# A guard at the end of a logsumexp kernel: range checks on the chip and a branch to a second path

## The chip, the cores and the metric

The kernel runs on one core of one Trainium2 chip. The metric is the device time of one execution in microseconds (us). The engines are TensorE (PE, with its weight loads PEld), VectorE (DVE), ScalarE (ACT), GpSimd (POOL) and SyncE (SP, which issues most DMAs).

## What is computed

```python
def reference(x, bias):          # x: (8, 2048, 2048) float32, bias: (8, 256) float32
    B, S, D = x.shape
    H = bias.shape[0]
    Dh = D // H
    x_heads = x.reshape(B, S, H, Dh).transpose(0, 2, 1, 3)
    x_heads = x_heads + bias[None, :, None, :]
    x_tiled = np.repeat(x_heads, 2, axis=2)
    mx = x_tiled.max(axis=-1, keepdims=True)
    lse = mx.squeeze(-1) + np.log(np.exp(x_tiled - mx).sum(axis=-1))
    return lse.astype(np.float32)          # (8, 8, 4096)
```

x and bias are drawn from a normal distribution. Each of the 16384 rows of x has 8 heads of 256 columns. For each head the kernel needs the log of the sum of exp(x + bias), and writes it twice. x is 134 MB, the result 1 MB.

## The kernel before

The kernel takes no maximum: it sums exp(x + bias) as it is and takes the log of the sum.

x comes in 64 tiles of 2 rows per partition (128 x 2 x 2048 numbers, 2 MB), 8 tiles to a batch. Four buffers (`xbs`) hold two tiles each. Tiles up to 41 are loaded in pairs (4 MB, L158), later ones alone, the last ones in pieces (L170). All loads are issued by SP, and the load of tile t + 8 waits until tile t's last users (`last_uses`, mostly DVE's reduce, L401) are done.

Every engine issues its instructions in the order in which the program writes them (`manual_schedule`). `STAGES` sets how a tile's heads are shared out.

- BULK (tiles 0 to 53). PE adds the bias to heads 0 to 2 in PSUM (L267 puts the bias there, L326 adds x through the identity). ACT takes exp of head 0 with its sum (L337) and of heads 1 and 2 (L344). POOL adds the bias to heads 4 to 7 in place (L376: 128x2048 numbers, x and `b_rep`, both in SBUF). ACT takes exp of heads 3 to 7 (L382). For heads whose exp was taken without the bias, DVE multiplies by exp(bias) (L394; the factors `w_ps` lie in PSUM). DVE then sums heads 1 to 7 (L401).
- MIXED (tiles 54 to 56) and the prompt stages (57 to 63). DVE multiplies by exp(bias) and sums one head at a time (L417, factors in `one_ps` and `w_ps` in PSUM, and once in `w_sb` in SBUF). POOL folds one or two heads (L433 multiplies by `w_sb`, L441 adds halves), and DVE sums what is left of them (L447).

The sums of batch b go to `R[b]`, 128 x 4 x 8 x 8 numbers of SBUF, 128x128 in all; those of the last batch to `R_last`. Two tiles after the last tile of a batch, `finish(b)` has PE transpose `R[b]` into the PSUM tile `tp` (L461) and ACT take the log into `res` (L471). After the seventh batch `store()` issues one store for seven batches (L475). At the end `finish_last()` transposes `R_last` (L482), takes the log (L488) and stores it (L489). Behind it, drains and semaphores close the program (L623).

The loop's end is where the change's calls hang:

```python
        fb, at = divmod(t - 2, NBLK)
        if fb >= 0 and at == NBLK - 1:
            finish(fb)
            if fb == B - 2:
                store()
    flush(for_pe)
    flush(for_pool)
    finish_last()
```

At loop step t DVE has been given the reduce of tile t - 1, so `finish(b)` comes on DVE behind the reduce of the tile that follows the batch.

The start: ACT loads the bias as one row (`brow`, L199), SP issues the first loads, POOL splits the bias into three bf16 parts (L208 to L212), ACT issues three small loads of them (L214), and DVE copies the spread bias to `b_rep` (L225).

Of the kernel before, what the change touches and what calls it, by code (L numbers as in the profile page):

```python
# [9 lines left out]
F32 = mybir.dt.float32  # L10
BF16 = mybir.dt.bfloat16
ACT = mybir.ActivationFunctionType
ALU = mybir.AluOpType
# [9 lines left out]
NEARLY = 5  # L23

NWARM = 3

# [27 lines left out]
def kernel(  # L56
# [6 lines left out]
    nc = tc.nc  # L63
    P = nc.NUM_PARTITIONS
    B, S, D = x.shape
    H, Dh = bias.shape
# [13 lines left out]
    sb = ctx.enter_context(tc.tile_pool(name="sb", bufs=1))  # L80
# [7 lines left out]
    ident = sb.tile([P, P], F32, name="ident")  # L88
# [2 lines left out]
    b3 = sb.tile([3, CPE], BF16, name="b3")  # L91
    bparts = sb.tile([1, 3, CPE], BF16, name="bparts")
    brest = sb.tile([1, 2, CPE], F32, name="brest")

    R = [sb.tile([P, KB, H, NB], F32, name=f"R{b}") for b in range(B - 1)]
    R_last = sb.tile([P, H, NBLK, K], F32, name="R_last")
    res = sb.tile([H * NB, B - 1, P, KB, 2], F32, name="res")
    res_last = sb.tile([P, P, 2], F32, name="res_last")
    xbs = [sb.tile([P, KB, D], F32, name=f"xb{i}") for i in range(NBUF // TB)]
# [6 lines left out]
    ps = [p[:, c : c + MM] for p in pairs for c in (0, MM)]  # L106
# [5 lines left out]
    def pieces(t):  # L112

        if len(modes_of(t)) == 1:
            return [(0, K, 0, D)]
        cols = [[(0, D)]] * K if t < T - 1 else LAST_COLS
        return [(k, k + 1, c0, c1) for k in range(K) for c0, c1 in cols[k]]
# [16 lines left out]
    def on_x(t, ins, after):  # L134
        buf = users[t // TB % len(xbs)]
        for t_u, u in buf:
            same = u.ins.engine == ins.ins.engine
            if u not in after and (not same or t_u % NBUF == t % NBUF and t_u < t):
                tc.declare_no_dep(
                    ins.ins,  # L140
                    u.ins,
                    reason="another tile, or waited for by those it waits for",
                )
        buf.append((t, ins))
        return ins
# [5 lines left out]
    def load(t):  # L151
        if TB <= t < BLOCKS:

            if t % TB == 0:
                after = [u for i in range(TB) if t >= NBUF for u in last_uses[t + i - NBUF]]
                ins = on_x(
                    t,
                    nc.sync.dma_start(  # L158
                        out=xbs[t // TB % len(xbs)], in_=rows_of(t, TB)
                    ),  # L160
                    after,
                )
                for i in range(TB):
                    loads[t + i, 0, 0] = ins
            return
        after = last_uses[t - NBUF] if t >= NBUF else []
        for k0, k1, c0, c1 in pieces(t):
            loads[t, k0, c0] = on_x(
                t,
                nc.sync.dma_start(  # L170
                    out=xts[t % NBUF][:, k0:k1, c0:c1],
                    in_=rows_of(t)[:, k0:k1, c0:c1],
                ),
                after,
            )
# [14 lines left out]
    for set_idx, (_name, funcs) in enumerate(get_activation_tables(nc.m.arch).items()):  # L190
        if ACT.Exp in funcs and ACT.Ln in funcs:
            nc.scalar.add_instruction(
                mybir.InstLoadActFuncSet(
                    name=nc.get_next_instruction_name(),
# [4 lines left out]
    nc.scalar.dma_start(out=brow, in_=bias.rearrange("h j -> (h j)").unsqueeze(0))  # L199
    for t in range(NBUF):  # L200
        load(t)
    nc.vector.memset(ones, 1.0)
    nc.vector.memset(ones3, 1.0)
    make_identity(nc, ident)

# [35 lines left out]
    n_ps = [0]  # L241
# [73 lines left out]
    def keep_warm():  # L315
        for _ in range(NWARM):
            nc.tensor.matmul(  # L317
                tp[:, 0], lhsT=ident, rhs=ident, start=True, stop=True
            )
# [45 lines left out]
    def each_row(src, c, n, k_rows):  # L365

        return bass.AP(
            tensor=src.tensor,
            offset=src.offset + c,
            ap=[src.ap[0], [0, k_rows], [1, n]],  # L370
        )
# [57 lines left out]
    def fold(t, k, h0, h1, sums, after):  # L429
# [24 lines left out]

        return add_up

    def finish(b):

        nr = H * NB
        for k in range(KB):  # L460
            nc.tensor.transpose(  # L461
                out=tp[0:nr, k],
                in_=R[b][:, k].rearrange("p h n -> p (h n)"),
                identity=ident,
            )
        tv = bass.AP(
            tensor=tp.tensor,
            offset=tp.offset,
            ap=[[tp.ap[0][0], nr], [1, P], [P, KB], [0, 2]],
        )  # L470
        nc.scalar.activation(out=res[:, b], in_=tv, func=ACT.Ln)  # L471
# [6 lines left out]
        )  # L478

    def finish_last():  # L480
        last = tp[:, KB - 1]
        nc.tensor.transpose(  # L482
            out=last, in_=R_last.rearrange("p h n k -> p (h n k)"), identity=ident
        )
        tv = bass.AP(
            tensor=last.tensor, offset=last.offset, ap=[last.ap[0], [1, P], [0, 2]]
        )
        nc.scalar.activation(out=res_last, in_=tv, func=ACT.Ln)  # L488
        nc.sync.dma_start(  # L489
            out=out[B - 1].rearrange("h (n r) -> (h n) r", r=2 * P),  # L490
            in_=res_last.rearrange("q p r -> q (p r)"),
        )


# [21 lines left out]
    def flush(later_work):  # L516
        for f in later_work:
            f()
        later_work.clear()

    for t in range(T):
        if t == T_FACTORS:
# [70 lines left out]
    flush(for_pe)  # L593
    flush(for_pool)
    finish_last()

    order.__exit__(None, None, None)

# [29 lines left out]
```

## Time and profile before

| what | value |
| --- | --- |
| time of three runs, us | 325.65, 325.32, 325.33 (median 325.33) |
| profiled execution: span from the first to the last instruction, us | 323.1 |
| median less that span, us (the page lists no other time of the profiled execution) | 2.2 |
| mean granted TensorE clock in it | 0.913 of full |
| read from and written to HBM, MB | 134.23, 1.05 |
| mean rate over the span, GB/s | 419 |
| POOL L376, 57 instructions, us busy | 257.6 |
| DVE L401, 56 instructions, us busy | 214.5 |
| ACT L382, 77 instructions, us busy | 157.1 |

How to read it: the page gives the busy time and the share of the span of each engine, then the span in 40 slices, where a digit is the busy share in tenths. Groups of instructions have a count, the busy time in us, the mean in ns of one, and the idle time of the engine before them with what ended it. In the chain of waits each line is a start in us, a length in us, and the engine, tile and line that the end of the program was waiting for at that time; "issue" is time in which the engine waited for nothing that the profile shows. In a timeline the first number is the start and the second the length.

### The profile page before, as it was taken

The numbers are of one execution on the slowest core, as the hardware profiler recorded it, in microseconds if no ns is written. First come the engines' busy times: TensorE is split into PE (matmuls) and PEld (weight loads), VectorE is DVE, ScalarE is ACT, GpSimd is POOL, SyncE is SP. The second block draws the span as 40 slices with busy tenths as digits, with TensorE's granted clock in tenths as the row PEclk, the third lists the DMA queues.
The fourth block names the chain that finished last, engine by engine and source line by source line (L and its number), as shares of the span: only waits on it lengthen the run. The fifth ranks groups of instructions, "written<-read, shape, count | busy, mean of one in ns | idle before, by whom it ended". The sixth has DMA issues, their size and how long they took to land.

```text
span 323.1 us, 2398 instructions
## 1 busy us (share of the span) xinstructions
PE 270.3 (84%) x691; PEld 102.9 (32%) x691; DVE 283.9 (88%) x306; ACT 265.8 (82%) x426; POOL 287.7 (89%) x120
## 2 busy tenths in 40 slices
PE   5999999889978769977869886888997786599984
PEld 2333333333323223322323322333333232035442
DVE  1037779999999998999899899898999999999995
ACT  1148679889869976988888978889998998899995
POOL 6939998999999999999999999999999999858874
PEclk9979799979979996998997997997999999559998
DMA  8999999999999999999999999999999999999995
GB/s 311 457 402 454 450 400 439 450 402 446 438 414 446 432 418 443 430 422 447 422 426 441 422 434 442 404 426 430 432 422 431 430 428 425 416 422 421 419 401 170
DMA packets 8830, 135.42 MB, mean 419 GB/s; under 512 B 1041, under 2 KB 1425, under 8 KB 2417
## 3 DMA queue, kind: packets, MB, share of 16 engines
q1 hardware_dynamic: 8720, 135.27, 98.6%
q8 instruction: 5, 0.08, 0.1%
q14 instruction: 7, 0.06, 0.0%
q10 hardware_dynamic: 98, 0.01, 0.0%
HBM read 134.23 MB, written 1.05 MB: 419 GB/s over the span
## 4 chain that ended last, share of the span: by engine, by line
DMA 40%; POOL 18%; ACT 17%; PE 14%; DVE 9%; issue 0%; SPq 0%; DVEq 0%
DMA xb<-in_x_dram 40%; POOL xb L376 18%; ACT xb L382 11%; DVE R L401 6%; PE pair L326 5%; PE one_ps L326 3%; PE pair L267 3%; ACT xb L357 2%; PE one_ps L267 2%; DVE xb L417 2%; PE pair L219 1%; ACT xb L337 1%; DVE xb L394 1%; ACT res L471 1%; ACT xb L344 1%; DMA brow<-in_bias_dram 1%
## 5 line engine op out<-in xcount | busy, mean ns | idle before, releaser
L376 POOL TENSOR_TENSOR xb<-xb,b_rep 128x2048 f32<-128x2048 f32 x57 | 257.6, 4539 | 20.7 <-DMA xb<-in_x_dram 20.6
L401 DVE TENSOR_REDUCE R<-xb 128x14 f32<-128x3584 f32 (+1 forms) x56 | 214.5, 3830 | 1.9
L382 ACT ACTIVATE xb<-xb 128x2560 f32<-128x2560 f32 (+5 forms) x77 | 157.1, 2050 | 10.3 <-POOL xb L376 10.1
L326 PE MATMUL pair<-xb,ident 128*128 128x512 f32 x216 | 114.3, 656 | 0.0
L326 PE MATMUL one_ps<-xb,ident 128*128 128x512 f32 x108 | 67.5, 710 | 11.5 <-DMA xb<-in_x_dram 11.5
L344 ACT ACTIVATE xb<-pair 128x1024 f32<-128x1024 f32 x54 | 55.5, 1027 | 23.2 <-PE pair L326 23.0
L326 PEld LDWEIGHTS pair<-xb,ident 128*128 128x128 f32 x216 | 46.2, 214 | 61.3 <-issue 61.3
L394 DVE TENSOR_TENSOR xb<-xb,w_ps 128x512 f32<-128x512 f32 x54 | 36.7, 681 | 26.2 <-ACT xb L382 26.2
L337 ACT ACTIVATE xb<-one_ps 128x256 f32<-128x256 f32 x108 | 40.0, 380 | 6.6 <-PE one_ps L326 6.6
L267 PEld LDWEIGHTS <-ones 3*128 3x128 bf16 (+1 forms) x192 | 16.9, 95 | 80.8 <-issue 71.4
L267 PE MATMUL one_ps<-b,ones 3*128 3x512 bf16 x49 | 18.6, 380 | 25.4 <-ACT xb L337 25.3
L267 PE MATMUL pair<-b,ones 3*128 3x512 bf16 x98 | 29.0, 375 | 0.0
L326 PEld LDWEIGHTS one_ps<-xb,ident 128*128 128x128 f32 x108 | 17.2, 200 | 33.9 <-DMA xb<-in_x_dram 18.0
L302 PE MATMUL pair<-xb,ident 128*128 128x512 f32 (+1 forms) x36 | 21.7, 689 | 5.7 <-DMA xb<-in_x_dram 5.7
L417 DVE CUSTOM_DVE_ANT_0 xb<-xb,w_ps 128x256 f32<-128x256 f32 x61 | 22.4, 418 | 0.0
L337 ACT ACTIVATION_READ_ACCUMULATOR xb<-one_ps 128x1 f32 x108 | 22.3, 207 | 0.0
L441 POOL TENSOR_TENSOR xb<-xb 128x128 f32<-128x128 f32 (+3 forms) x39 | 13.8, 355 | 3.1
L433 POOL TENSOR_TENSOR xb<-xb,w_sb 128x256 f32<-128x256 f32 (+1 forms) x13 | 10.0, 771 | 5.2 <-ACT xb L382 4.5
L317 PE MATMUL tp<-ident 128*128 128x128 f32 x84 | 13.7, 302 | 0.0
L317 PEld LDWEIGHTS tp<-ident 128*128 128x128 f32 x84 | 11.1, 200 | 3.5 <-issue 3.0
L357 ACT ACTIVATE xb<-pair 128x256 f32<-128x256 f32 x33 | 11.9, 364 | 0.0
L417 DVE CUSTOM_DVE_ANT_0 xb<-xb,one_ps 128x256 f32<-128x256 f32 x27 | 10.6, 415 | 0.1
(42 smaller groups left out, 83.4 us busy)
## 6 DMA issues: line engine op xcount, KB each, us to landing
xb<-in_x_dram SPq DMA_DIRECT2D x20, 4096.0 KB, 21.5
xb<-in_x_dram SPq DMA_DIRECT2D x17, 2048.0 KB, 22.7
xb<-in_x_dram SPq DMA_DIRECT2D x12, 1024.0 KB, 22.7
xb<-in_x_dram SPq DMA_DIRECT2D x4, 256.0 KB, 13.2
out_dram<-res SPq DMA_DIRECT2D x1, 896.0 KB, 6.7
xb<-in_x_dram SPq DMA_DIRECT2D x2, 384.0 KB, 15.8
xb<-in_x_dram SPq DMA_DIRECT2D x2, 128.0 KB, 6.3
out_dram<-res_last SPq DMA_DIRECT2D x1, 128.0 KB, 1.7
```

Of the source, the lines that this page charges most:

```text
L267: nc.tensor.matmul(p, lhsT=lhsT, rhs=each_row(b, h * Dh, Dh, K), start=i == 0, stop=False,)
L302: mm = nc.tensor.matmul(p, lhsT=ident, rhs=xts[t % NBUF][:, ka:kb, c : c + w], start=False, stop=True,)
L317: nc.tensor.matmul(tp[:, 0], lhsT=ident, rhs=ident, start=True, stop=True)
L326: mm = nc.tensor.matmul(p, lhsT=ident, rhs=xts[t % NBUF][:, :, h * Dh : (h + 1) * Dh], start=False, stop=True,)
L337: act = nc.scalar.activation(out=xts[t % NBUF][:, k, 0:Dh], in_=got[0][:, k * Dh : (k + 1) * Dh], func=ACT.Exp, accum_out=sums[:, k, 0:1],)
L344: act = nc.scalar.activation(out=xts[t % NBUF][:, :, Dh : m["pe"] * Dh].rearrange("p k (h j) -> p h k j", j=Dh), in_=got[-1].rearrange("p ...
L357: act = nc.scalar.activation(out=xts[t % NBUF][:, k, h * Dh : (h + 1) * Dh], in_=p, func=ACT.Exp, accum_out=sums[:, k, h : h + 1],)
L376: add = nc.gpsimd.tensor_tensor(out=v, in0=v, in1=each_row(b_rep, c - G0, D - c, k1 - k0), op=ALU.add)
L382: return on_x(t, nc.scalar.activation(out=v, in_=v, func=ACT.Exp), [after])
L394: mul = nc.vector.tensor_tensor(out=f, in0=f, in1=each_row(w_ps, m["pe"] * Dh - W0, n, k1 - k0), op=ALU.mult,)
L401: red = nc.vector.tensor_reduce(out=sums[:, k0:k1, h0:H], in_=v.rearrange("p k (h j) -> p k h j", j=Dh), op=ALU.add, axis=mybir.AxisListTy ...
L417: ttr = nc.vector.tensor_tensor_reduce(out=v, in0=v, in1=w, scale=1.0, scalar=0.0, op0=ALU.mult, op1=ALU.add, accum_out=dst,)
```

## The change

At the start the bias is loaded a second time, as 128 rows of 16 numbers, and DVE compares it with -32 and 32. In `finish(b)` DVE compares the 128x128 sums of the batch with 1e-12 and 1e18 and adds the outcome (1 where a value was changed by the clamp) to `bad`. In `finish_last()` it does the same for the last batch; PE counts `bad` and `out_of` over the partitions by two matmuls with a column of ones, and DVE sums the 128 counts to one number, `flag`. SP, ACT and DVE read `flag` into a register and branch. Where it isn't zero, `general()` computes all again with the maximum: 32 rounds, each loading 4 MB of x. With the inputs drawn here the sums and the bias lie inside the bounds.

```diff
+B_MAX = 32.0
+S_MIN, S_MAX = 1e-12, 1e18
+GB = 4
+GENERAL_B = 2
...
+    b_flat = sb.tile([P, D // P], F32, name="b_flat")
+    held = sb.tile([P, P], F32, name="held")
+    out_of = sb.tile([P, P], F32, name="out_of")
+    bad = sb.tile([P, P], F32, name="bad")
+    ones_k = sb.tile([P, 1], F32, name="ones_k")
+    flag = sb.tile([1, 1], F32, name="flag")
...
     nc.scalar.dma_start(out=brow, in_=bias.rearrange("h j -> (h j)").unsqueeze(0))
     for t in range(NBUF):
         load(t)
+    nc.scalar.dma_start(
+        out=b_flat, in_=bias.rearrange("h j -> (h j)").rearrange("(p c) -> p c", p=P)
+    )
     nc.vector.memset(ones, 1.0)
+    nc.vector.memset(ones_k, 1.0)
+    nc.vector.memset(bad, 0.0)
     nc.vector.memset(ones3, 1.0)
...
+    def outside(v, lo, hi, to):
+
+        c = held[:, 0 : v.shape[-1]]
+        nc.vector.tensor_scalar(
+            out=c, in0=v, scalar1=lo, scalar2=hi, op0=ALU.max, op1=ALU.min
+        )
+        nc.vector.tensor_tensor(out=to, in0=c, in1=v, op=ALU.not_equal)
+
+    def check_sums(r):
+        outside(r, S_MIN, S_MAX, out_of)
+        nc.vector.tensor_tensor(out=bad, in0=bad, in1=out_of, op=ALU.add)
+
     def finish(b):
 
+        check_sums(R[b].rearrange("p k h n -> p (k h n)"))
         nr = H * NB
...
     def finish_last():
+        r_last = R_last.rearrange("p h n k -> p (h n k)")
+        outside(r_last, S_MIN, S_MAX, out_of)
         last = tp[:, KB - 1]
         nc.tensor.transpose(
-            out=last, in_=R_last.rearrange("p h n k -> p (h n k)"), identity=ident
-        )
+            out=last, in_=r_last, identity=ident
+        )
+        count = ps[n_ps[0] % len(ps)][0:1, 0:P]
+        nc.tensor.matmul(count, lhsT=ones_k, rhs=bad, start=True, stop=False)
+        nc.tensor.matmul(count, lhsT=ones_k, rhs=out_of, start=False, stop=True)
...
         nc.sync.dma_start(
             out=out[B - 1].rearrange("h (n r) -> (h n) r", r=2 * P),
             in_=res_last.rearrange("q p r -> q (p r)"),
+        )
+        nc.vector.tensor_reduce(
+            out=flag, in_=count, op=ALU.add, axis=mybir.AxisListType.X
+        )
+
+    def general():
+
+        bias_all = xbs[GENERAL_B]
+        nc.sync.dma_start(
+            out=bias_all[:, 0],
+            in_=bass.AP(tensor=bias.tensor, offset=bias.offset, ap=[[0, P], [1, D]]),
+        )
...
+        for n, g in ((n, g) for n in range(S // P) for g in range(B // GB)):
...
+            nc.sync.dma_start(out=v, in_=xs[n, :, g * GB : (g + 1) * GB])
...
+    outside(b_flat, -B_MAX, B_MAX, bad[:, 0 : D // P])
 
     for t in range(T):
         if t == T_FACTORS:
...
     finish_last()
+    found = nc.values_load(
+        flag.bitcast(mybir.dt.int32),
+        engines=[mybir.EngineType.SP, mybir.EngineType.Activation, mybir.EngineType.DVE],
+        skip_runtime_bounds_check_because="only compared with zero",
+    )
+    with tc.If(found != 0, preferred_fallthrough_block=False):
+        general()
 
     order.__exit__(None, None, None)
```

In each round of `general()`, which is left out above, SP loads and stores, DVE adds the bias, takes the maximum, subtracts it and sums, and ACT takes exp and the log: on DVE five instructions a round, on ACT two, on SP two DMAs.

## What was predicted before the run

> **What bounds the kernel now.** I read the page first: busy shares and the slices.
>
> ```profile
> PE 270.3 (84%) x691; PEld 102.9 (32%) x691; DVE 283.9 (88%) x306; ACT 265.8 (82%) x426; POOL 287.7 (89%) x120
> ...
> DMA  8999999999999999999999999999999999999995
> ```
>
> The DMA engines are full from the second slice to the last but one, so the kernel is bound by reading x. Four compute engines are 82 to 89% busy under it: an instruction added to one of them is free only where that engine has a wait to give up. The change adds to VectorE (DVE) above all, so I went on to the waits, of the whole span, then of 230 to 304 us, then from 304 us.
>
> ```profile
> DVE xb L394 <- ACT xb L382: 26.2, 15, 12.6
> ```
> ```profile
> DVE xb L394 <- ACT xb L382: 0.2, 1, 0.2
> ```
> ```profile
> DVE R_last L447 <- POOL xb L441: 0.7, 4, 0.2
> ```
>
> Columns: waited in all, times, longest. DVE's 26.2 us are 12.6 before its first tile and 13.6 spread over the loop, yet in 230 to 304 us it waits once, 0.15 us at 230.25; after that it has its next work ready until 305 us. Then come four waits for POOL's folds (0.15, 0.20, 0.20, 0.19 us at 305.38, 307.46, 309.55, 311.63). So a delay of DVE before 230 us dies in a wait; one after 230 us is carried to 305 us, loses at most 0.74 us there, and goes on to the end. The chain of waits shows that DVE is the path from there:
>
> ```profile
> 312.54 1.60 ACT xb L382
> 314.14 0.02 issue
> 314.16 0.42 DVE xb L417
> ...
> 319.50 0.14 DVE R_last L447
> 319.64 0.14 issue
> 319.78 0.32 PE tp L482
> 320.09 0.02 issue
> 320.11 0.38 ACT res_last L488
> ```
>
> From 314.16 to 319.64 every link is DVE; then the transpose, Ln and the last store. At 314.16 DVE waits some 0.03 us for ACT's exp: 0.77 us of slack in all. Last, SP's own waits:
>
> ```profile
> SPq L489 <- ACT res_last L488: 6.5, 1, 6.5
> SPq L623 <- DMA out_dram<-res_last: 1.2, 1, 1.2
> ```
>
> The store is issued at 320.52, lands 1.7 us later (322.2), and the closing drains and semaphores end at 323.1, 0.9 us after the landing. While the store flies nothing else runs: cover of 1.7 us for anything that starts early enough.
>
> **The change part by part.** The sum is made against the profiled execution: span 323.1 us. The median of the three runs is 325.33, 2.2 us more, which I take as what lies around the span and leave alone.
>
> *The start.* Two memsets (0.165 us the like), a bias load of 128 rows of 64 bytes on ACT's queue and two compares on 128x16. DVE waits 12.57 us before its first tile at 21.15, and ACT until 9.45; both take this up. The three small loads behind it (L214) took 5.8 us to land and are first needed from the sixth tile on, after 38 us. Even if the bias needs as long, it is there by 8 us. Were the cover gone, it would cost about 1 us. The bytes: the like small queue (q10) shows 98 packets at 0.0%, so below 0.05% of 16 x 323 us, below 0.026 us each; 128 of them are below 0.2 us of DMA time. Taken as 0.
>
> *The checks.* Each of the seven finish() calls puts three 128x128 instructions on DVE: clamp, compare, add. The trace has none of that size, so by the neighbours:
>
> ```profile
> L394 DVE TENSOR_TENSOR xb<-xb,w_ps 128x512 f32<-128x512 f32 x54 | 36.7, 681 | 26.2 <-ACT xb L382 26.2
> L417 DVE CUSTOM_DVE_ANT_0 xb<-xb,w_ps 128x256 f32<-128x256 f32 x61 | 22.4, 418 | 0.0
> L447 DVE TENSOR_REDUCE R_last<-xb 128x1 f32<-128x32 f32 x12 | 2.2, 185 | 0.7 <-POOL xb L441 0.7
> ```
>
> From 681 ns for 512 columns and 418 for 256: 1.03 ns a column, so 418 - 132 = 286 ns for 128. The reduces agree: 185 ns for 32 columns plus 96 x 1.04 is 285. A dependent successor starts 0.03 us after the end (L394 to L401: 0.72 start to start for 0.69), an independent one 0.08 us before it (L417: 0.34 for 0.42). One check: 0.315 + 0.315 + 0.205 = 0.84 us. Bounds: 0.62 if all three overlap by 0.08; above, the port rival below.
>
> Where they fall: the check of a batch stands on DVE behind the reduce of the tile after it, so behind the L401 that end at 68.1, 104.5, 143.6, 181.8, 220.2 and 257.4 us; the seventh stands about 296.1 us among the L417. The first five meet waits of DVE (0.17 and 0.79 at 99.9 and 105.3, 2.01 at 130.0, 1.00 at 158.2, 0.31 to 0.79 at 172 to 183, 1.25 at 206.5, 0.79 at 221.0, 0.15 at 230.25) and die there. The loads wait for DVE's reduce, and one issued 0.84 us later lands no later: a 4 MB load lands 21.5 us after its issue (median), about 10 us of which are its own bytes at 419 GB/s, so about 11 us of older bytes stand before it. The sixth and the seventh have no wait behind them but the 0.77 us: 2 x 0.84 - 0.77 = **0.91 us** later on DVE at 314.16, hence at the store. Bounds: 0.47 (0.62 us a check) and 1.7 (slack gone).
>
> *The flag.* With the shift, the last L447 ends at 320.54. The transpose, Ln and store don't wait for what is new: issue 321.43, landing 323.1. Beside them: two more DVE instructions (0.03 + 0.286 + 0.03 + 0.286) to 321.17; the matmul that counts, priced as L482 (0.45 from DVE's end to PE's end) to 321.62; the reduce of 128 numbers, 0.03 + 0.285, to 321.94. Then SP, ACT and DVE each read the word into a register and branch. No row shows either. Below, a semaphore instruction of the closing block (0.02 us); above, the bias load at the start, 2.05 us from issue to landing (0.77 to 2.82). I take the middle, 1.0, as both are one round trip to a memory but the load also builds descriptors; for the branch 0.2, between 0.02 and 0.46 (the longest drain); and 0.2 for semaphores set right where the paths meet (some eight of 28 ns). That ends at 323.34, 0.24 later than the landing; bounds -1.1 (hidden: 0) and +1.4. Taken: **0.3 us**.
>
> Sum: 0.9 + 0.3 = +1.2 us, span 324.3, time **326.5 us**; with these bounds 325.8 to 328.4.
>
> On the flag the Trainium skill (Runtime: NRT & Kernel Launch, Instruction fetch mechanics) gives about 200 ns for a register loaded; as an estimate by that page the flag hides under the store and the time is 326.2. The same section warns that a taken branch to code outside the fetched window stalls; that is the second rival.
>
> **Rivals.**
> 1. *POOL stands in DVE's way.* Before the change, no DVE instruction of the main loop has both inputs in SBUF: L394 and L417 take weights from PSUM tiles (w_ps, one_ps). The sole exception:
>
> ```profile
> L417 DVE CUSTOM_DVE_ANT_0 xb<-xb,w_sb 128x256 f32<-128x256 f32 x1 | 0.4, 422 | 0.0
> ```
> ```profile
> 253.68 9.03 POOL L376 TENSOR_TENSOR xb<-xb,b_rep 128x2048 f32<-128x2048 f32 x2
> ```
>
> It starts at 319.07, POOL's last ends at 319.17, and it takes 422 ns as its kind does: 0.1 us of overlap, no sign of a wait, but little proof. The checks run wholly in SBUF while POOL is inside such 4.5 us instructions. Lighter form: each check waits once for the instruction that runs. At 257.4 that has 0.76 us left: 327.3 at least. With half an instruction (2.27) at each of six checks: 6 x 3.11 + 0.84 - 8.5 (DVE's waits from 99.9 on, 0.77 included) = 11.0, plus 0.3: 336.6. Heavy form: each of the three waits a whole POOL instruction: 0.76 + 2 x 4.54 + 0.84 = 10.7 a check; 6 x 10.7 + 0.84 - 8.5 = 56.5, DVE becomes the bound: 382. For: all three operands in SBUF, POOL 89% busy. Against: that one row.
> The Trainium skill (SBUF — State Buffer, Who interferes with whom) says DVE with two SBUF inputs, or in a mode using both ports, shares a port pair with GpSimd, and the later of the two is blocked fully until the other ends. By that page, as an estimate, the sum would be this rival's heavy form. The one overlapping row doesn't show it, and no other row here can.
> 2. *The branch waits for code.* The page's queues q8 and q14 bring instructions by DMA while the kernel runs. If the next code on SP, ACT or DVE isn't there, a small transfer's 2.05 us comes on top, once or twice: 328.6 to 330.6. For: 32 rounds of another path lie in the code. Against: the untaken path is asked to follow directly.
> 3. *Not slower.* The two late checks cost some 0.52 us each (0.206 for each that overlaps, the clamp half of that), and the flag hides under the store's 1.7 us. It decides if a check costs below 0.66 us and read and branch below 1.1 us: shift 0 to 0.55, 325.3 to 325.9.
> 4. *The other path runs after all.* Sums of 256 exponentials of normal numbers lie far inside 1e-12 to 1e18, a bias far below 32. It would read x again, 32 x 4 MB at 419 GB/s: over 320 us more.
>
> **How the numbers follow.** Forecast, 326.0 to 328.4: 0.42. Rival 2, to 330.6: 0.15. Rival 1 light, 327.3 to 336.6: 0.20; heavy, to 382: 0.13. Rival 3: 0.09; rival 4 or anything faster: 0.01. Leaving out the heavy form, rival 4 and the top of the lighter one, the range is 325.3 to 335. A measurement of this kernel can tell about 0.2% (0.65 us) from no change: slower 0.90, same 0.09, faster 0.01.
>
> **What would show it.** Right: clamp, compare and add rows of 0.2 to 0.3 us; no DVE wait from 257 to 305 us and fewer than four L447 waits after; the last L447 ends near 320.5; less than 0.5 us between the store's landing and SP going on. Wrong: rows of the checks lasting 1 to 5 us and ending with a POOL instruction (rival 1), POOL's L376 above 4.54; an empty stretch of 2 us or more behind the branch with an instruction packet in it (rival 2); a shorter SP wait for the store with the end unmoved (rival 3).

## The result and the profile after

The changed kernel takes 347.75 us (median of four runs, 346.52 to 348.04), the kernel before 325.32 us beside it. The ratio is 1.0675, with a 95% interval of 1.0655 to 1.0696: 22.4 us more, where 1.2 had been predicted, and above the predicted range (up to 335 us). The span is 345.8 us (323.1 before). So 22.7 us must be found in the trace. The lines of the loop have moved: L398 is POOL's addition of the bias (L376 before), L416 DVE's multiply (L394), L423 DVE's reduce (L401), L404 ACT's exp (L382), L469 DVE's small reduce of the tail (L447), L482 the clamp, L485 the compare, L489 the add.

The page after, its engines and the DMA slices:

```profile
PE 271.0 (78%) x695; PEld 103.0 (30%) x695; DVE 317.2 (92%) x334; ACT 263.5 (76%) x426; POOL 287.7 (83%) x120
...
DMA  8999999999999999999999999999999979999500
```

The other engines are as busy as before to within 2.3 us; DVE has 33.3 us more. The DMA slices are no longer all full: in the last quarter reading x waits for something. The chain of waits by engine says for what; the kernel before comes first, then the changed one:

```profile
DMA 40%; POOL 18%; ACT 17%; PE 14%; DVE 9%; issue 0%; SPq 0%; DVEq 0%
```
```profile
DVE 78%; PE 15%; ACT 4%; issue 1%; DMA 1%
```

The mean granted TensorE clock is lower too, 0.879 for 0.913, but PE is busy only 0.7 us longer and has 15% of the chain for 14%.

The groups of DVE by form show what the 33.3 us are (count, busy us, mean ns, idle time before them):

```profile
L482 DVE TENSOR_SCALAR held<-R 128x128 f32<-128x128 f32 x7 | 14.8, 2117 | 0.0
L489 DVE TENSOR_TENSOR bad<-bad,out_of 128x128 f32<-128x128 f32 x7 | 10.6, 1521 | 0.2
L485 DVE TENSOR_TENSOR out_of<-held,R 128x128 f32<-128x128 f32 x7 | 6.5, 935 | 0.2
...
L485 DVE TENSOR_TENSOR out_of<-held,R_last 128x128 f32<-128x128 f32 x1 | 0.3, 293 | 0.0
...
L482 DVE TENSOR_SCALAR held<-R_last 128x128 f32<-128x128 f32 x1 | 0.2, 227 | 0.1
```

The same clamp and compare, on the same size, take 227 and 293 ns on the sums of the last batch, when POOL has finished, and 2117 and 935 ns on average inside the loop. The seven checks take 14.8 + 10.6 + 6.5 = 31.9 us, 4.56 us each. That the profile counts it as busy time doesn't mean that DVE computes for so long: the 2 us are a stand inside an instruction that has started. To see what ends it, two checks on DVE's timeline and POOL's line beside them (start, length):

```profile
67.34 4.52 DVE L482 TENSOR_SCALAR held<-R 128x128 f32<-128x128 f32 x1
71.90 0.29 DVE L485 TENSOR_TENSOR out_of<-held,R 128x128 f32<-128x128 f32 x1
72.22 0.29 DVE L489 TENSOR_TENSOR bad<-bad,out_of 128x128 f32<-128x128 f32 x1
```
```profile
62.74 9.03 POOL L398 TENSOR_TENSOR xb<-xb,b_rep 128x2048 f32<-128x2048 f32 x2 [0.61 <-DMA xb<-in_x_dram]
72.40 4.55 POOL L398 TENSOR_TENSOR xb<-xb,b_rep 128x2048 f32<-128x2048 f32 x1 [0.63 <-DMA xb<-in_x_dram]
```

POOL's second instruction ends at 62.74 + 9.03 = 71.77 us, DVE's clamp at 71.86. POOL then waits 0.63 us for its next tile, and in that pause compare and add run at their own lengths. The fifth check meets a POOL that doesn't pause:

```profile
225.24 1.13 DVE L482 TENSOR_SCALAR held<-R 128x128 f32<-128x128 f32 x1
226.40 4.53 DVE L485 TENSOR_TENSOR out_of<-held,R 128x128 f32<-128x128 f32 x1
230.97 4.52 DVE L489 TENSOR_TENSOR bad<-bad,out_of 128x128 f32<-128x128 f32 x1
```
```profile
212.74 40.68 POOL L398 TENSOR_TENSOR xb<-xb,b_rep 128x2048 f32<-128x2048 f32 x9
```

Nine POOL instructions follow each other without a pause (4.52 us each), and now compare and add each last one of them. This check costs 10.2 us, from 225.24 to the start of the next multiply at 235.41.

The same holds in all the kernels below that have such instructions in the loop. Over seven profiles 62 of them last longer than 0.6 us, and each of the 62 ends 0.08 to 0.16 us behind the end of one of POOL's additions of the bias. DVE's own waits show what became of the cover that the prediction counted on:

```profile
DVE xb L416 <- ACT xb L404: 13.0, 5, 7.1
```

Before it was 26.2 us. 7.1 us of the 13.0 are before the first tile and the rest ends at 44.8 us; behind that DVE never waits in the loop, so all later delay is carried on. The last reduce of tile 55 ends at 309.8 us, 21.3 after that of the kernel before (288.5). The remaining 1.4 us arise behind it, nearly all behind the last store: from its issue to the end it is 3.77 us (2.62 before).

### The profile page after: what moved, and what is told of

It reads as the page before. It is cut to its first block, busy times and chain, and to the rows that moved or that the text cites. A ratio compares the mean times of both kernels' runs of the same rounds, so it can differ in the third digit from the quotient of the medians.

```text
span 345.8 us, 2458 instructions
## 1 busy us (share of the span) xinstructions
PE 271.0 (78%) x695; PEld 103.0 (30%) x695; DVE 317.2 (92%) x334; ACT 263.5 (76%) x426; POOL 287.7 (83%) x120
## 4 chain that ended last, share of the span: by engine, by line
DVE 78%; PE 15%; ACT 4%; issue 1%; DMA 1%
DVE R L423 52%; DVE xb L439 9%; DVE xb L416 8%; PE pair L348 6%; DVE held L482 4%; DVE bad L489 3%; PE one_ps L348 3%; PE pair L289 3%; ACT xb L404 3%; DVE out_of L485 2%; PE one_ps L289 2%; PE pair L241 1%; DVE R_last L423 1%; ACT xb L366 1%; DMA brow<-in_bias_dram 1%
## 5 line engine op out<-in xcount | busy, mean ns | idle before, releaser
L398 POOL TENSOR_TENSOR xb<-xb,b_rep 128x2048 f32<-128x2048 f32 x57 | 257.6, 4539 | 22.2 <-DMA xb<-in_x_dram 22.2
L423 DVE TENSOR_REDUCE R<-xb 128x14 f32<-128x3584 f32 (+1 forms) x56 | 214.5, 3830 | 1.9
L404 ACT ACTIVATE xb<-xb 128x2560 f32<-128x2560 f32 (+5 forms) x77 | 158.2, 2066 | 2.6 <-POOL xb L398 2.6
L348 PE MATMUL pair<-xb,ident 128*128 128x512 f32 x216 | 117.2, 671 | 0.0
L366 ACT ACTIVATE xb<-pair 128x1024 f32<-128x1024 f32 x54 | 56.9, 1054 | 18.8 <-PE pair L348 18.7
L416 DVE TENSOR_TENSOR xb<-xb,w_ps 128x512 f32<-128x512 f32 x54 | 36.7, 679 | 13.0 <-ACT xb L404 13.0
L359 ACT ACTIVATE xb<-one_ps 128x256 f32<-128x256 f32 x108 | 41.2, 402 | 5.8 <-PE one_ps L348 5.7
L289 PE MATMUL one_ps<-b,ones 3*128 3x512 bf16 x49 | 18.7, 382 | 21.3 <-ACT xb L359 21.3
L496 PE MATMUL tp<-ident,R 128*32 128x128 f32 x28 | 6.7, 335 | 35.4 <-DVE R L423 35.4
L506 ACT ACTIVATE res<-tp 32x1024 f32<-32x1024 f32 x7 | 7.1, 1012 | 33.5 <-PE tp L496 33.5
L455 POOL TENSOR_TENSOR xb<-xb,w_sb 128x256 f32<-128x256 f32 (+1 forms) x13 | 10.0, 772 | 21.9 <-ACT xb L404 21.3
L348 PEld LDWEIGHTS one_ps<-xb,ident 128*128 128x128 f32 x108 | 17.4, 203 | 25.4 <-issue 19.1
L359 ACT ACTIVATION_READ_ACCUMULATOR xb<-one_ps 128x1 f32 x108 | 24.8, 230 | 0.0
L324 PE MATMUL pair<-xb,ident 128*128 128x512 f32 (+1 forms) x36 | 18.4, 595 | 0.0
L463 POOL TENSOR_TENSOR xb<-xb 128x128 f32<-128x128 f32 (+3 forms) x39 | 13.8, 355 | 3.1
L482 DVE TENSOR_SCALAR held<-R 128x128 f32<-128x128 f32 x7 | 14.8, 2117 | 0.0
L496 PEld LDWEIGHTS tp<-ident,R 128*32 128x32 f32 x28 | 1.8, 101 | 40.3 <-DVE R L423 38.2
## 6 DMA issues: line engine op xcount, KB each, us to landing
xb<-in_x_dram SPq DMA_DIRECT2D x4, 256.0 KB, 10.7
```

The source lines that it names most:

```text
L289: nc.tensor.matmul(p, lhsT=lhsT, rhs=each_row(b, h * Dh, Dh, K), start=i == 0, stop=False,)
L324: mm = nc.tensor.matmul(p, lhsT=ident, rhs=xts[t % NBUF][:, ka:kb, c : c + w], start=False, stop=True,)
L348: mm = nc.tensor.matmul(p, lhsT=ident, rhs=xts[t % NBUF][:, :, h * Dh : (h + 1) * Dh], start=False, stop=True,)
L359: act = nc.scalar.activation(out=xts[t % NBUF][:, k, 0:Dh], in_=got[0][:, k * Dh : (k + 1) * Dh], func=ACT.Exp, accum_out=sums[:, k, 0:1],)
L366: act = nc.scalar.activation(out=xts[t % NBUF][:, :, Dh : m["pe"] * Dh].rearrange("p k (h j) -> p h k j", j=Dh), in_=got[-1].rearrange("p ...
L398: add = nc.gpsimd.tensor_tensor(out=v, in0=v, in1=each_row(b_rep, c - G0, D - c, k1 - k0), op=ALU.add)
```

## The theories and the experiments

The letters in the expectations: **P** is the first rival of the prediction, POOL stands in the way of the checks on DVE, which then is the bound. **B** says that the time comes with the branch and the second path's code. **C** says that PE and ACT, which keep the order in which the program is written, stand behind a late finish(), and that this multiplies the delay. Of P there are forms: that only instructions with two inputs in SBUF stand; or (P2, in the last kernels) that every DVE instruction wholly in SBUF but the reduces does, and that the clamp alone can stand over several POOL instructions. The kernel before was run beside each group of kernels: 325.43, 325.21 and 325.40 us.

### Without the seven checks

```diff
     def finish(b):
-        check_sums(R[b].rearrange("p k h n -> p (k h n)"))
```

The sums of the first seven batches are not compared with the bounds; the flag, the branch and the second path stay.

> The seven checks in the loop are left out (the sums of the first seven batches aren't compared); the bias check, the check of the last batch, the count, the flag and the branch stay. Theory P (a check's DVE instruction, with all operands in SBUF, stands until POOL's running instruction ends; DVE has no waits left after about 45 us, so 31.9 us of checks less some 8.5 us of waits reach the end): the checks were nearly all of it, what stays is the end: store to end 3.8 us in place of 2.6 us, so 326.5 to 327.2 us. Rival B (the branch, its second path's code and the flag cost it): 340 us or more.

Measured: 326.44 us (326.0 to 327.84), ratio 1.0032 (1.0019 to 1.0046), just below what P expected. Of 22.4 us some 21 go with 21 small DVE instructions. B falls as the main cause; what is left over the kernel before is about 1 us.

### Without the branch

```diff
-    found = nc.values_load(
...
-    with tc.If(found != 0, preferred_fallthrough_block=False):
-        general()
```

The checks and the flag are computed and nobody reads the flag; the second path isn't there.

> The checks stay, the flag is computed, but nobody reads it: register loads, branch and second path are left out. Theory P: only the end gets shorter, by the 1.2 us that it took over the store's landing: 346 to 346.8 us, with the same long check instructions. Rival B: back to within 5 us of the kernel before.

Measured: 345.55 us (345.18 to 345.92), ratio 1.0617 (1.0592 to 1.0642), 2.2 below the changed kernel. That is a little below the expected 346 to 346.8. The three groups of the checks take 31.0 us (13.8, 10.6 and 6.6) for 31.9; if that is 0.9 of the difference, the rest, 1.3 us, goes with the branch. B falls a second time, from the other side.

### The same checks when POOL is done

```diff
     def finish_last():
+        for r in R:
+            check_sums(r.rearrange("p k h n -> p (k h n)"))
...
```

(and no call in finish()).

> The same seven checks, instruction for instruction, all moved behind the last sum of the last batch, when POOL has nothing left to do. Theory P: each takes its own length, 0.23 + 0.29 + 0.29 us and gaps, so 21 instructions take about 6 us; they stand before the last batch's check but not before its store; with the end of 1.2 us, of which the store now hides more, 330 to 333 us. Rival C or a theory by which the instructions are slow by themselves (2.1 us the clamp, 1.5 us the add): 21 instructions of 32 us, 355 us or more.

Measured: 329.85 us (329.65 to 330.76), ratio 1.014 (1.0114 to 1.0167), just below what P expected. DVE's groups by form:

```profile
L485 DVE TENSOR_TENSOR out_of<-held,R 128x128 f32<-128x128 f32 x7 | 2.0, 292 | 0.2
L489 DVE TENSOR_TENSOR bad<-bad,out_of 128x128 f32<-128x128 f32 x7 | 2.0, 292 | 0.2
L482 DVE TENSOR_SCALAR held<-R 128x128 f32<-128x128 f32 x7 | 1.5, 219 | 0.0
```

The same 21 instructions on the same data take 5.5 us in place of 31.9, so neither their work nor the addresses make them long. They cost 3.4 us more than no checks at all (326.44), as the last store, issued at 319.04 us, flies beside part of the 5.5. PE, ACT and the loads are done there too, so this run alone doesn't name POOL; the ends of the 62 instructions do, and the next experiment keeps the place. The 3.4 us are the price of a place without POOL and without cover, a sixth of the loss.

### A reduce in place of clamp, compare and add

```diff
-        check_sums(R[b].rearrange("p k h n -> p (k h n)"))
+        r = R[b].rearrange("p k h n -> p (k h n)")
+        for i, op in enumerate((ALU.max, ALU.min)):
+            nc.vector.tensor_reduce(
+                out=ends[:, i, b : b + 1], in_=r, op=op, axis=mybir.AxisListType.X
+            )
+        if b == B - 2:
+            outside(
+                ends.rearrange("p i b -> p (i b)"),
+                S_MIN,
+                S_MAX,
+                bad[:, D // P : D // P + 2 * (B - 1)],
+            )
...
```

Per batch DVE takes the largest and the smallest sum of each partition, and compares these 14 columns once.

> Each check becomes two reduces on DVE, maximum and minimum of the same 128x128 sums into one column each, and the columns are compared once after the seventh batch. The reduces read one operand in SBUF. Theory P: they don't wait for POOL, 0.29 us each whatever POOL does; two late checks of 0.5 us less 0.77 us of slack reach the end, and the 1.2 us of the end: 326.5 to 327.5 us. Rival C (any DVE instruction put in at this place costs as much, since PE and ACT stand behind it with the transposes and the log): still 340 us or more, with PE waiting tens of us for the reduces as it does now (38 us at the transposes).

Measured: 326.69 us (326.27 to 328.62), ratio 1.0042 (1.0026 to 1.0058). The reduces read the same `R[b]` in the same places of the loop:

```profile
L496 DVE TENSOR_REDUCE ends<-R 128x1 f32<-128x128 f32 x14 | 3.3, 276 | 0.0
```

Fourteen of them, none longer than 279 ns, by the side of 2117 for the clamp; eleven run wholly inside one of POOL's additions. DVE's multiply, which writes 128x512 numbers to SBUF and has one operand in PSUM, is as unharmed: none of the 54 in the changed kernel lasts longer than 690 ns, and 34 lie wholly inside an addition of POOL. So it isn't SBUF, the place or `R` that stands in the way, but the kind of the instruction. This is the best version with the guard that was run.

### The reduces without the branch

The kernel above without the register reads, the branch and the second path.

> Maximum and minimum as before, but nobody reads the flag: register loads, branch and second path are left out. What is left is the reduces: 2 late checks of 0.5 us less 0.77 us of slack, so 0.2 to 0.4 us over the kernel before, 325.4 to 325.9 us; the branch itself is then worth 0.9 to 1.3 us of the 326.7 us. If the time stays at 326.5 us or more, the reduces or the start cost it and not the branch.

Measured: 325.74 us (325.27 to 327.59), ratio 1.0016 (1.0001 to 1.0031). Against their own runs of the kernel before, the reduces cost 0.3 us and the guard as a whole 1.3; so branch and flag are about 0.9 us of it.

### Marks in bf16 and an earlier count

```diff
-    out_of = sb.tile([P, P], F32, name="out_of")
-    bad = sb.tile([P, P], F32, name="bad")
+    out_of = sb.tile([P, P], BF16, name="out_of")
+    bad = sb.tile([P, P], BF16, name="bad")
...
-    ones_k = sb.tile([P, 1], F32, name="ones_k")
+    ones_k = sb.tile([P, 1], BF16, name="ones_k")
...
+        nc.tensor.matmul(count, lhsT=ones_k, rhs=bad, start=True, stop=False)
         last = tp[:, KB - 1]
...
```

This is meant to bring the flag of the kernel with the reduces forward.

> As the kernel with maximum and minimum, and with a shorter way to the flag: the marks and the column of ones are bf16, and the matmul that counts the earlier marks stands before the last transpose. Theory: the two counting matmuls took 1.2 us on PE with the last one ending 0.9 us after the last mark; with one pass each and only one of them late, the flag comes 0.5 to 0.8 us earlier and the end with it: 326 to 326.8 us. If the end doesn't move, something other than the flag sets it (the semaphores where the paths meet, or the store).

Measured: 326.76 us (326.19 to 328.2), ratio 1.0041 (1.0026 to 1.0055): no gain. In the profiles the time from the last store's issue to the end is 3.53 us for 3.72, so the flag came some 0.2 us earlier where 0.5 to 0.8 was expected; a difference of that size doesn't show in the times.

### finish() two tiles later

```diff
-        fb, at = divmod(t - 2, NBLK)
+        fb, at = divmod(t - 4, NBLK)
```

PE's transposes wait 35.4 us for DVE in the changed kernel and ACT's logs 33.5 us for PE; before, the logs waited 4.1. C makes these waits a cause; here they have two tiles of time.

> The checks as changed, but each finish (check, transposes, log) two tiles later. Rival C (the loss comes from PE and ACT standing in order behind transposes that wait for DVE's late sums, 38 us on PE): two tiles more give DVE 9 us to get there, most PE and ACT waits go, and the time falls by 8 us or more. Theory P: DVE is the bound from 45 us on without waits, so what PE and ACT wait for costs nothing: 345 to 350 us, PE's wait for the sums much smaller, the check instructions as long as before on average (they meet other POOL instructions, so a few us either way).

Measured: 347.47 us (346.91 to 348.79), ratio 1.0695 (1.0669 to 1.072). The checks take 31.3 us. PE's transposes now wait 11.6 us and ACT's logs 14.7, and the time stays: these waits come from DVE's stand and cost nothing of their own, and C falls.

### The checks on POOL

```diff
...
-        outside(r, S_MIN, S_MAX, out_of)
-        nc.vector.tensor_tensor(out=bad, in0=bad, in1=out_of, op=ALU.add)
+        c = held_g[:, 0 : r.shape[-1]]
+        nc.gpsimd.tensor_scalar(
+            out=c, in0=r, scalar1=S_MIN, scalar2=S_MAX, op0=ALU.max, op1=ALU.min
+        )
+        nc.gpsimd.tensor_tensor(out=out_g, in0=c, in1=r, op=ALU.subtract)
+        nc.gpsimd.tensor_tensor(out=out_g, in0=out_g, in1=out_g, op=ALU.mult)
+        nc.gpsimd.tensor_tensor(out=bad_g, in0=bad_g, in1=out_g, op=ALU.add)
...
+        nc.tensor.matmul(count, lhsT=ones_k, rhs=bad_g, start=False, stop=False)
```

Four instructions on POOL (clamp, subtract, square, add) take the place of the three on DVE; a difference that isn't zero counts as outside. In the loop DVE then has no instruction of the kind that stands.

> [...] POOL takes about 0.46 us for a 128x128 two-operand instruction in the trace, so 1.9 us a check, and waits 22 us in all for x. Theory P: DVE has no instruction that POOL can hold up; POOL's waits take the checks up: 326.5 to 328.5 us. Rival C: POOL is 83 to 89% busy too and stands before ACT, so most of 7 x 1.9 us comes through: 335 us or more.

Measured: 330.2 us (329.79 to 332.22), ratio 1.0171 (1.0136 to 1.0206), above what was expected. POOL's waits of the loop in this kernel:

```profile
POOL xb L402 <- DMA xb<-in_x_dram: 8.0, 4, 4.9
...
POOL held_g L493 <- DVE R L427: 1.9, 1, 1.9
```

POOL had 20.6 us of waits for loads before and gives up only 12.6 of them, for 13.6 us of instructions, their gaps and a wait for DVE's reduce: the waits of an engine are not all to be had. In this execution the last store is issued 2.4 us later than before (322.94 for 320.52). The other half of the loss lies behind the store: 5.06 us to the end where the changed kernel has 3.77 and the kernel before 2.62 (see the second rival below). The loss is 5 us instead of 22, as P has it.

### POOL's addition in halves

```diff
...
-        v = xts[t % NBUF][:, k0:k1, c:D]
-        add = nc.gpsimd.tensor_tensor(
-            out=v, in0=v, in1=each_row(b_rep, c - G0, D - c, k1 - k0), op=ALU.add
-        )
+        for k in range(k0, k1):
+            v = xts[t % NBUF][:, k : k + 1, c:D]
+            add = nc.gpsimd.tensor_tensor(
+                out=v, in0=v, in1=each_row(b_rep, c - G0, D - c, 1), op=ALU.add
+            )
...
```

If a check waits for the POOL instruction that runs, half as long an instruction should halve the wait.

> The checks as changed, but POOL's bias add of 128x2048 is split into two instructions of 128x1024 (2.3 us each). Theory P, that the wait is for the whole POOL instruction that runs: no check instruction lasts over 2.6 us (now up to 4.6 us), the checks' sum falls from 31.9 to between 14 and 22 us, the time to 330 to 340 us, if POOL's own total doesn't grow by more than 5 us. Rival D (the two engines share a port word by word, or DVE is slow at such operands by itself): check instructions keep their lengths, 345 us or more.

Measured: 359.21 us (357.09 to 360.56), ratio 1.1056 (1.103 to 1.1082): the opposite of what was expected. At 225 us it goes as P has it, with 2.36 and 2.33 us for compare and add where one POOL instruction takes 2.36. But the sixth check:

```profile
267.79 19.59 DVE L484 TENSOR_SCALAR held<-R 128x128 f32<-128x128 f32 x1
287.41 0.29 DVE L487 TENSOR_TENSOR out_of<-held,R 128x128 f32<-128x128 f32 x1
```
```profile
219.92 67.37 POOL L399 TENSOR_TENSOR xb<-xb,b_rep 128x1024 f32<-128x1024 f32 x29
```
```profile
L399 POOL TENSOR_TENSOR xb<-xb,b_rep 128x1024 f32<-128x1024 f32 x114 | 265.7, 2363 | 12.9 <-DMA xb<-in_x_dram 12.9
```

One clamp stands for 19.59 us, more than eight POOL instructions of 2.36 us, and is let go at 287.4 us. POOL's last instruction of an unbroken row of 29, from 219.92 us on, ends at 287.29; the check at 225 us, which was let in at each end, lies in the same row. So an end of a POOL instruction isn't always a door for DVE. The time alone would suit rival D of the expectation, but the lengths don't: the other eight long instructions of the loop last 1.8 to 2.4 us and each ends with one of POOL's. The checks take 41.5 us in all, 9.6 more than in the changed kernel, and the profiled execution is 9.6 us longer (357.09 for 347.54; the medians differ by 11.5). POOL itself does 8.1 us more work (265.7 for 257.6), as two halves take 2 x 2.363 = 4.73 us for 4.54.

### Three compares, or three clamps

```diff
-        outside(r, S_MIN, S_MAX, out_of)
-        nc.vector.tensor_tensor(out=bad, in0=bad, in1=out_of, op=ALU.add)
+        for c in (held, out_of, held):
+            nc.vector.tensor_tensor(out=c, in0=ident, in1=r, op=ALU.not_equal)
```
```diff
+        for c in (held, out_of, held):
+            nc.vector.tensor_scalar(
+                out=c, in0=r, scalar1=S_MIN, scalar2=S_MAX, op0=ALU.max, op1=ALU.min
+            )
```

The seven checks are replaced by instructions of one kind whose outcome nobody uses: three with two inputs in SBUF, or three with one.

> A check is three compares of the sums with the identity, two operands in SBUF each; clamp and add are left out, and nothing of the first seven batches is marked. Theory P2 (an instruction of this kind waits for the end of the POOL instruction that runs, never for a second one): no compare over 4.6 us; the first of a check waits for a rest, the others 0.29 us where POOL pauses or a whole instruction where it has work ready; sum 20 to 45 us, time 336 to 360 us. If only the clamp did harm: below 330 us.

> A check is three clamps, one operand in SBUF each and two constants; compare and add are left out, and nothing of the first seven batches is marked. Theory P2: the clamp waits for POOL as well, though it reads one operand, and it is the one that can miss the gap between two POOL instructions (19.6 us once where POOL's adds were halved): at least one clamp over 4.6 us, 340 us or more. If what counts is two operands in SBUF alone: 0.22 us each, below 328 us.

Measured: 342.01 us (341.78 to 342.66), ratio 1.0519 (1.0502 to 1.0537), with compares; 341.87 us (341.46 to 342.81), ratio 1.0506 (1.0488 to 1.0523), with clamps. The groups of the kernel with three compares come first, then those of the kernel with three clamps:

```profile
L489 DVE TENSOR_TENSOR held<-ident,R 128x128 f32<-128x128 f32 x14 | 21.0, 1503 | 0.0
...
L489 DVE TENSOR_TENSOR out_of<-ident,R 128x128 f32<-128x128 f32 x7 | 6.3, 898 | 0.0
```
```profile
L489 DVE TENSOR_SCALAR held<-R 128x128 f32<-128x128 f32 x14 | 22.8, 1628 | 0.0
L482 DVE TENSOR_SCALAR held<-b_flat 128x16 f32<-128x16 f32 x1 | 7.5, 7487 | 1.8 <-DMA b_flat<-in_bias_dram 1.8
...
L489 DVE TENSOR_SCALAR out_of<-R 128x128 f32<-128x128 f32 x7 | 5.9, 838 | 0.0
```

Both kinds stand alike, 27.3 and 28.7 us in all. That only two inputs in SBUF make an instruction stand falls: the clamp has one. None of the clamps of the checks lasts longer than 4.6 us, though P2 had expected one that does; only the clamp of the bias at the start does, on 16 columns, and there the cover of DVE's first wait hides it. Its row with POOL's above it, in the kernel with three clamps:

```profile
9.03 8.96 POOL L398 TENSOR_TENSOR xb<-xb,b_rep 128x2048 f32<-128x2048 f32 x2
10.54 7.49 DVE L482 TENSOR_SCALAR held<-b_flat 128x16 f32<-128x16 f32 x1 [1.76 <-DMA b_flat<-in_bias_dram]
```

It passes the end of POOL's first addition (13.52 us) and is let go at that of the second. So with whole additions too an instruction can stand over more than the one that runs. The same clamp lies in all thirteen changed kernels: in the five where POOL goes on without a pause it takes 7.4 to 7.6 us, in the eight where POOL pauses between its first two tiles, by 0.09 us or more, 2.2 to 2.8 us.

### Three compares beside the halves

Both edits together.

> The three compares, and POOL's bias add in two instructions of 128x1024 (2.36 us). Theory P2: no compare over 2.5 us, so the sum is at most 6 x 3 x 2.4 and likely 20 to 30 us, and the time lies below that of the three compares with whole adds by 3 us or more, without the 19.6 us that the clamp stood. If the wait isn't for one POOL instruction: some compares over 2.5 us, or no less time.

Measured: 356.28 us (356.08 to 359.48), ratio 1.0986 (1.0934 to 1.1038). The sixth check again:

```profile
267.43 19.62 DVE L491 TENSOR_TENSOR held<-ident,R 128x128 f32<-128x128 f32 x1
286.97 0.28 DVE L491 TENSOR_TENSOR out_of<-ident,R 128x128 f32<-128x128 f32 x1
```

A compare stands 19.62 us in the place where the clamp did, where 2.5 us at most had been expected, and the time is 14 us above that of the three compares with whole additions, not 3 below. P2 falls in this point: the clamp isn't special, and a second POOL instruction can be waited for. In both kernels with halves it is the first instruction of the sixth check that stands so long; what decides is open (see below).

## Why the prediction was wrong, step by step

**The step that failed is the price of one check**, "0.315 + 0.315 + 0.205 = 0.84 us", and with it the chances: the forecast got 0.42 and the rival that came about 0.33 in two forms. As a price of the instructions alone it was right: 219 + 292 + 292 = 803 ns where POOL is done. Inside the loop a check took 4.56 us on average. The rows that it was worked out from could not show this: L394 and L417 have an operand in PSUM, and L447 is a reduce, the very kinds that don't stand. The prediction named this, and then let one row speak against it ("no sign of a wait, but little proof"): an overlap of 0.1 us at the end of a POOL instruction. By what the runs show, an instruction that starts in the last 0.1 us of POOL's would wait 0.1 us and look as long as ever; with halves, a clamp that starts at 67.33 us, 0.14 us before the end of one of POOL's, takes 0.22 us.

**The rival's mechanism was right, its size lay between its two forms.** Its sign in the prediction, rows of 1 to 5 us that end with a POOL instruction, is what the trace shows; POOL's own instruction isn't longer (4539 ns before and after). The light form has 3.11 us a check, the heavy one 10.7; measured are 5.1, 2.5, 2.9, 2.8, 10.2 and 7.1 us for the first six, from the start of the clamp to that of the next multiply. Which of the two a check gets is decided by POOL: where it waits 0.6 us for the next tile, compare and add slip into the pause (light form, checks one to four), and where its tiles have landed ahead, each of them waits a whole instruction (heavy form, check five). At the sixth POOL pauses 0.35 us: the compare gets in, the add stands 4.60 us. The seventh meets POOL's short folds and takes 1.4.

The Trainium skill (SBUF — State Buffer, Who interferes with whom) says that DVE and GpSimd share one pair of ports, taken for a whole instruction by the one that issues first while the other is fully blocked; that DVE needs it with two SBUF inputs or in a two-port mode, which a `tensor_scalar`, the clamp's kind, can enter; and that on this chip a reduce never does. On the kinds the runs agree: 4.53 us for a compare, up to 4.58 for a clamp in the loop, 276 ns for a reduce. That the clamp runs in such a mode no row shows. On who goes next they don't agree everywhere: by its record the clamp with halves started at 267.79 us, ahead of POOL's instruction of 268.73, and yet it stood until 287.38; there the measurement decides. As an estimate by that page the prediction had the heavy form for all checks, 382 us; measured, with POOL's pauses, are 347.75.

**The cover was counted rightly, and was too small.** "A delay of DVE before 230 us dies in a wait" holds for 0.84 us a check. The sum of the waits from 99.9 us on, slack included, was 8.5 us; the first two checks alone take 7.6. With the durations that were measured the rival's sum reads 30.5 + 1.4 - 8.5 = 23.4 us on DVE, for 21.3 measured at the end of tile 55. The seventh check (1.4) and the slack (0.77) lie behind that point, and the first tile's multiply starts 0.65 us earlier than before; of the rest, 0.8 us, the cause is open. The seventh check is taken up: from the end of tile 55's reduce to the store's issue the two kernels take 32.0 and 32.2 us.

**The loads** were said to land no later for a DVE that is late by 0.84 us, as older bytes stand before them. For 21 us this can't hold, and the slices after 230 us show it: DMA is 0.96 busy at 393 GB/s from 230 to 305 us, before 1.01 at 424. The kernel is then bound by DVE, and reading x follows.

**The start** was taken as 0: right. The bias check took 2.4 us and ended at 13.35, and the first tile's multiply started at 20.50, before that 21.15.

**The flag and the branch** were taken as 0.3 us, with bounds 0 and 1.4; the kernels with and without the branch differ by 0.9 (reduces) and 1.3 us (checks). From the last store's issue to the end it is 2.54 to 2.62 us in the three profiles without a branch and 3.72 to 3.78 in seven of those with one. The trace of the changed kernel has the register reads, once on each engine (lengths in ns, then the first and last start):

```profile
L684 SPq TENSOR_LOAD <-flag x1: 466/466/466, 342.8 to 342.8; - x1
L684 ACTq TENSOR_LOAD <-flag x1: 474/474/474, 342.8 to 342.8; - x1
L684 DVEq TENSOR_LOAD <-flag x1: 540/540/540, 342.8 to 342.8; - x1
```
```profile
L689 SPq EVENT_SEMAPHORE  x8: 17/17/17, 343.5 to 344.0; - x8
L689 SPq COMPARE_BRANCH  x2: 37/43/49, 343.4 to 344.0; - x2
```

SP is through at 344.06, 0.39 us after the store has landed (issued at 341.98, 1.7 in flight), where 0.24 was predicted. That it came so near is luck, as errors cancel: the read is 0.5 us where 1.0 was taken, PE ends the count 0.86 us behind the last mark where 0.45 was taken, and branch and semaphores take some 0.8 where 0.4 was. What had no term in the sum is the block behind it. Before, the closing drains and semaphores ended 0.9 us after the landing, since they had begun beside the store; now they start behind the branch and take 1.7 us from 344.06 to the end. In the last 6 us the page's queue q14 also brings three packets of instructions, which the kernel before doesn't have there. Whether these packets make the closing longer wasn't tried.

**The second rival**, a branch that waits for code, isn't what makes the 22 us (326.44 without checks). But something like it can be seen in two profiles of other kernels, without checks and with the checks on POOL. In the first DVE's second branch is at 320.9 us and its next drain at 323.4, with instruction packets between; in that with the reduces the drain follows in 0.6 us. From the last store's issue to the end the two take 5.22 and 5.06 us, 1.3 to 1.5 more than the changed kernel. Both have no small DVE instructions in the loop, so the branch lies elsewhere in DVE's code; whether that is the reason wasn't tried. The execution without checks took 326.01 us all the same, at the low end of its kernel's runs (326.0 to 327.84), as its store was issued 1.5 us earlier than before (319.01); why, no run shows.

**That the sum of the stands is the time** can be held against all kernels. Where the small DVE instructions are in the loop, their sums and the time of the same profiled execution above the median of the kernel before are:

| kernel | sum of the checks on DVE, us | time above before, us |
| --- | --- | --- |
| reduces, with the one clamp and compare behind them | 4.1 | 1.0 |
| three compares | 27.3 | 16.5 |
| three clamps | 28.7 | 17.4 |
| checks, no branch | 31.0 | 19.9 |
| finish() two tiles later | 31.3 | 21.7 |
| the change | 31.9 | 22.2 |
| halves, three compares | 42.3 | 30.7 |
| halves, checks | 41.5 | 31.9 |

From the second row down, sum less time is 10.8, 11.3, 11.1, 9.6, 9.7, 11.6 and 9.6 us, and where there is a branch some 1 us for flag and branch is to be added: 10.6 to 12.6 us of stands that cost nothing, where the waits in the loop and the slack gave 8.5 and the seventh check 1.4 more. So the sums explain the times within about 3 us; what is over isn't settled.

**What stays open.** Why in both kernels with halves an instruction of DVE stood over eight POOL instructions at 267 us, while at 225 us, with POOL just as unbroken, each end of an instruction let DVE in. Whether the load for POOL's next instruction has landed doesn't separate the two: with halves it had landed at 222.75 us for the instruction of 226.87, where DVE was let in, and at 266.50 for that of 268.73, where it wasn't. Nor is it a matter of the halves alone, as the clamp of the bias shows at the start. Where POOL pauses, DVE was let in each time.

## What to carry to other kernels

Before a small instruction is put on VectorE, ask not only for its length but whether a long GpSimd instruction runs beside it, and whether its kind is one that the trace shows beside GpSimd unharmed: rows with an operand in PSUM and reduces say nothing about an elementwise instruction wholly in SBUF. Such an instruction mostly costs up to the length of the neighbour's, however little it does, and where the neighbour goes on without a pause it can cost several such lengths. So the same test should be written as a reduce (here 1.3 us in place of 22.4, guard included) or put where GpSimd is done. And sum the neighbour's price against the engine's waits in the order of time: the first checks use them up, and each later one is paid in full.

## What was not expected of the hardware

- Cutting the GpSimd instruction in two made it worse: a DVE instruction can stand over a whole row of them (19.6 us over more than eight of 2.36 us), not only over the one that runs.
- A clamp with one input, on 16 columns, stood 7.4 to 7.6 us in the five kernels where POOL went from its first addition to the second without a pause, and 2.2 to 2.8 us in the eight where it paused.
- A register read from SBUF took 0.47 to 0.71 us over the kernels, a compare with branch 37 to 55 ns; the closing behind a branch, 1.7 us, and 3.1 to 3.2 in two kernels, was dearer than both.
